# A two-layer diffusion backbone: the first projections by contraction tile, the second MLP half on normalised input, the output stores on two queues

## The chip, the cores and the metric

The kernel runs on 1 core of a Trainium2 chip. The metric is device time in microseconds (us) from the first to the last instruction of a launch, as a median of 3 runs: 902.71 us before (902.44 to 903.71). About 0.2% (1.8 us) is what a measurement of this kernel can tell from no change.

## The reference

384 tokens (128 context, 256 latent) of width 1024 pass two layers. In each layer, for both token groups with their own modulation vectors:

```
mod = silu(c) @ w_mod[d] + b_mod[d]          # six vectors of 1024: sa, ca, ga, sm, cm, gm
h   = rmsnorm(x, norm_mix) * (1 + ca) + sa
q, k, v, gb, gc, xin, u, vs = split(h @ w_in[d])
x  += ga * (concat(diff_attention, gated_conv, chunk_mlp) @ w_out[d])
h   = rmsnorm(x, norm_mlp) * (1 + cm) + sm
x  += gm * (relu(h @ w_up[d])**2 @ w_down[d])   # hidden width 4096
```

A last RMSNorm gives the outputs `y`; the context keys and values of both layers are outputs too. All weights are float32 in HBM.

## The kernel before

**Products.** Every weight tile (128 x 1024 float32, 512 KB) is loaded into a ring of six `raw` buffers, rounded by ScalarE to `whi` (L201), and VectorE puts the rest into `wlo` (L203). Activations lie transposed, as 8 tiles `kt` of 128 features by 384 tokens, in the same two pieces (`hh`, `hl`). One product is then three matmuls (`mm3`, L220 to L222). `whi` and `wlo` have four buffers each.

**Two kinds of `hh`, `hl`.** "Raw" input is `x` times its per-feature scale, without the norm's factor `rstd`, which is multiplied in after the product; the shift vector is carried as two more columns (TE = 386), so that its product comes with the others as a bias. "Normed" input has norm and shift in it (`normed`, L355). Both have a row pitch of 386 elements, whether 384 or 386 columns are read. The first projections of a layer and all up projections of the MLP read raw input; the other projections read normed input. In the MLP (two halves f of 16 hidden tiles: up `pup`, then down `pdn`), `hidden` takes the bias columns to `ub`, multiplies by `rstd` on VectorE, then has ReLU with bias, square and rounding on ScalarE.

**The modulation vectors.** The vectors of layer 0 but the last come from TensorE (`mod_products`: `pm` from `raw` and `sct`, L262), the rest from VectorE (`mod_sums`, `junk`, 112 products of 128 x 1024, L315). The first one (the scale of layer 0's norm) is needed before anything can be projected; it is made in 4 parts of two feature tiles.

**The start.** Key and query of heads 0 and 1 (four accumulators `pkq`) are built first: four whole weight tiles are loaded and split, then two feature tiles at a time are scaled as the parts of the vector come, and each accumulator takes its products for these two. Products of the next vectors stand between them.

**The order.** Engines run their own streams in the order in which the Python code records instructions. Side work is kept as generators: a heap releases a step when a counter of "ticks" (one for each product of three matmuls) has come far enough; the table `WAIT` holds the distances, a pair for the two layers. SyncE (SP) issues all loads and stores; its order is left to the scheduler.

**Softmax, layer by layer.** `attention(h, u)`: scores `sc` (three PSUM buffers `misc` shared with the transposes `pt`), negated maxima `nm` (VectorE), exponentials `e` (ScalarE), scaling and combining (`s`, `e`), transposes `pt`, copies `ats`, value products `po`. Beside it `keys` and `queries` rotate and split: `rt`, `kh`, `qs` and `kl`.

**The end.** The last down tile is done for latent tokens (256 columns) and then for context tokens (128): residual (L969), square, mean over features (`pstat`), ScalarE's logarithm and exponential, a refinement (L341 to L343), then four multiplies of two feature tiles each (three on VectorE, one on GpSimd, L988), each stored by SP (L989).

Of the kernel before, what the change touches and what calls it, by code (L numbers as in the profile page):

```python
# [9 lines left out]
F32 = mybir.dt.float32  # L10
# [5 lines left out]
P = 128  # L16
# [14 lines left out]
PARTS = 4  # L31
# [4 lines left out]
    "sums_down": (5, 0),  # L36
    "hid0": (1, 3),
    "hid1": (3, 4),
    "later": (4, 4),
    "later2": (4, 6),  # L40
    "spread": (1, 0),
    "final": (4, 3, 3, 3),
    "rstd": (3, 10),
# [4 lines left out]
    "at4": (5, 5),  # L48
    "at5": (1, 3),
    "at6": (2, 2),  # L50
    "at7": (3, 3),
    "at8": (2, 3),
    "at9": (2, 2),
    "at10": (3, 4),
    "at11": (2, 1),
    "at12": (2, 3),
    "k0": (1, 3),
    "k1": (9, 6),
    "k2": (1, 3),
    "q0": (1, 1),  # L60
    "q1": (5, 6),
    "q2": (2, 4),
    "fh0": (8, 14),
    "fh1": (2, 5),
    "fh2": (2, 2),
    "fh3": (5, 5),
    "cv0": (1, 5),
    "cv1": (2, 2),
    "cv2": (2, 3),
    "cm0": (1, 1),  # L70
    "sy": (4, 1),
    "normed": (3, 3),
    "wait_normed": (2, 12),
    "mix": (4, 4),
    "heads": (4, 1),
    "mods": (7, 0),
    "mods0": (2, 1),
    "sums": (7, 0),
    "sums0": (61, 1),
# [21 lines left out]
def dit_kernel(ctx, tc, xT, cT, wmod, wmodT, wall, ck, cv, ws, lam, bs_in, small, rope, ident_in, yT, kT_out, v_out):  # L101
# [10 lines left out]

    ahead = wpool.tile([P, 1024], F32, tag="raw", name="raw", bufs=6)
    nc.sync.dma_start(ahead, wmod[0, 0])
    c_sb = const.tile([P, KT, 2], F32, name="c_sb")
    nc.sync.dma_start(c_sb, cT)
# [130 lines left out]
    def mod_products():  # L247

        for i, (d, v) in enumerate(MOD_PE):
            pm = ps.tile([P, 256], F32, tag="mod", name="pm", bufs=1)  # L250
            tr = work.tile([P, KT, 32], F32, name="tr", tag="rtmp", bufs=1)

            n = per = PARTS if i == 0 else 1
            width = 256 // n
            for f in range(n):
                own = slice(f * width, f * width + width)
                for q in range(KT // per):
                    w = ahead if (i, f, q) == (0, 0, 0) else raw_chunk(wmod[i, f * KT // per + q])
# [10 lines left out]
                    if n > 1 or q % 2 == 1:  # L269
                        yield  # L270
                dts = slice(f * KT // n, (f + 1) * KT // n)
# [4 lines left out]
    hh = const.tile([P, KT, TE], F32R, name="hh")  # L276
    hl = const.tile([P, KT, TE], F32R, name="hl")
# [78 lines left out]
    def normed(scale, shift, every):  # L356
# [11 lines left out]
        for dt in range(KT):  # L368
            for g, a, b in GROUPS:
                nc.scalar.activation(hh[:, dt, a:b], t[:, a:b], AF.Identity, bias=shift[:, dt, g : g + 1])  # L370
            ahead = times(dt + 1) if dt + 1 < KT else None
            for g, a, b in GROUPS:
                nc.vector.scalar_tensor_tensor(
                    hl[:, dt, a:b], t[:, a:b], shift[:, dt, g : g + 1], hh[:, dt, a:b].bitcast(F32),
                    ALU.add, ALU.subtract,
                )
# [4 lines left out]
    def scaled_high(dt, scale):  # L381

        for g, a, b in GROUPS:
            nc.scalar.activation(hh[:, dt, a:b], x[:, dt, a:b], AF.Identity, scale=scale[:, dt, g : g + 1])

    def scaled_low(dt, scale):
        for g, a, b in GROUPS:
            nc.vector.scalar_tensor_tensor(  # L388
                hl[:, dt, a:b], x[:, dt, a:b], scale[:, dt, g : g + 1], hh[:, dt, a:b].bitcast(F32),
# [67 lines left out]
    def shift_products(raws, bias, t0, t1):  # L457
# [3 lines left out]
        for r in range(2):  # L461
            for j in range(4):
                kt = 4 * r + j
                mm(pb[32 * j : 32 * j + 32, 0 : n * P], sh[:, kt, :], raws[:, t0:t1, kt * P : kt * P + P],
# [44 lines left out]
    for d in range(DEPTH):  # L509
        lay = d * S_LAYER  # L510
        wt = {name: waits[d] for name, waits in WAIT.items() if len(waits) == DEPTH}
        a = (hh, hl)
# [26 lines left out]
        if d == 0:  # L539
            raws = wpool.tile([P, 2 * NPRE[d], 1024], F32, tag="hidH", name="raws")  # L540
            w2 = [refill(raws[:, i]) for i in range(2 * NPRE[d])]
            spread = spread_silu()

            def load_raw(i):
                nc.sync.dma_start(raws[:, i], wall[i])

            def split(i):
                next(w2[i])
                next(w2[i], None)

            def scaled(dt):
                scaled_high(dt, amix[d])
                scaled_low(dt, amix[d])
# [4 lines left out]
            next(products)  # L558
            nc.sync.dma_start(sm, small)
            next(products)  # L560
            load_raw(0)
            load_x(0)
# [549 lines left out]
```

## Time and profile before

| | |
|---|---|
| median of 3 runs | 902.71 us (902.44 to 903.71) |
| profiled execution, own time | 903.88 us |
| its span, first to last instruction | 902.1 us |
| TensorE busy | 876.5 us (97%) |
| VectorE, ScalarE, GpSimd busy | 653.7, 479.6, 83.5 us |
| mean granted clock of TensorE | 0.994 |

Rows of the windows view give, for a stretch in us from the span's start, its length and each engine's busy time with its instruction count, then the granted TensorE clock (1.00 is full), the DMA engines' busy share and GB/s. Timeline rows give start, duration, engine, line, operation and tiles, and in brackets the idle time of the engine before it and what ended it. Group rows end in busy time and mean duration in ns.

### The profile page before, as it was taken

The page shows a single profiled execution, that of the slowest core. Times are in us where ns is not written, and L with a number is a line of the kernel's source. Part 1 is how long each engine was busy: PE and PEld are TensorE (multiplying, and loading weights), DVE is VectorE, ACT ScalarE, POOL GpSimd, SP SyncE. Part 2 cuts the span into 40 slices and gives each one's busy share as a digit, 9 for nine tenths or more (in the row PEclk, how much of TensorE's full clock was granted, in tenths as well). Part 3 has the DMA queues.
Part 4 walks back from the last instruction along what each step waited for, and adds up shares of the span by engine and source line. Part 5 has one row for each costly group of instructions (what it writes and reads, how often), then busy time and mean ns, then how long its engine had stood idle before and what let it go on. Part 6 is the DMA issues. An engine that isn't in the chain of part 4 may idle for free.

```text
span 902.1 us, 14515 instructions
## 1 busy us (share of the span) xinstructions
PE 876.5 (97%) x5476; PEld 843.3 (93%) x5476; DVE 653.7 (72%) x1214; ACT 479.6 (53%) x949; POOL 83.5 (9%) x84
## 2 busy tenths in 40 slices
PE   5999999999999999999999989999999999999996
PEld 4877889999999999999997889999999999999995
DVE  4698888899888878889979877568886344554433
ACT  4568665547652236653446777545765223665331
POOL 1014210030000000000112430002000000000021
PEclk9999999999999999999999999999999999999998
DMA  9887784455656665566763323233555433333302
GB/s 342 318 310 261 250 277 169 137 165 189 208 191 231 211 211 183 187 204 216 230 199 123 111 81 110 95 109 127 192 201 166 134 123 120 137 118 121 113 1 70
DMA packets 48470, 156.55 MB, mean 174 GB/s; under 512 B 5392, under 2 KB 11024, under 8 KB 48400
## 3 DMA queue, kind: packets, MB, share of 16 engines
q1 hardware_dynamic: 48400, 155.63, 51.4%
q8 instruction: 43, 0.70, 0.3%
q14 instruction: 27, 0.22, 0.1%
HBM read 152.98 MB, written 2.62 MB: 172 GB/s over the span
## 4 chain that ended last, share of the span: by engine, by line
PE 86%; DVE 6%; ACT 3%; issue 2%; DMA 1%; POOL 1%; SPq 0%; DVEq 0%; ACTq 0%; POOLq 0%
PE pdn L221 10%; PE pdn L222 10%; PE pdn L220 10%; PE pup L221 10%; PE pup L220 10%; PE pup L222 9%; PE po L222 2%; PE po L221 2%; PE po L220 2%; PE pm L262 2%; PE pkq L220 2%; PE pkq L221 2%; DVE wlo L203 2%; PE pkq L222 1%; PE po L786 1%
## 5 line engine op out<-in xcount | busy, mean ns | idle before, releaser
L201 ACT CAST whi<-raw 128x1024 fp32r<-128x1024 f32 x182 | 190.1, 1051 | 302.9 <-PE pdn L221 154.0
L203 DVE TENSOR_TENSOR wlo<-raw,whi 128x1024 fp32r<-128x1024 f32 x182 | 223.6, 1234 | 63.6 <-ACT whi L201 63.5
L220 PE MATMUL pdn<-ah,whi 128*128 128x384 f32 (+2 forms) x528 | 174.7, 331 | 0.0
L221 PE MATMUL pdn<-al,whi 128*128 128x384 f32 (+2 forms) x528 | 174.6, 331 | 0.0
L222 PE MATMUL pdn<-ah,wlo 128*128 128x384 f32 (+2 forms) x528 | 174.6, 331 | 0.0
L220 PE MATMUL pup<-hh,whi 128*128 128x386 f32 x512 | 174.2, 340 | 0.0
L221 PE MATMUL pup<-hl,whi 128*128 128x386 f32 x512 | 173.7, 339 | 0.3
L222 PE MATMUL pup<-hh,wlo 128*128 128x386 f32 x512 | 172.8, 338 | 0.0
L315 DVE SCALAR_TENSOR_TENSOR junk<-raw,cb 128x1024 bf16<-128x1024 f32 x112 | 137.4, 1227 | 0.4
L221 PEld LDWEIGHTS pdn<-al,whi 128*128 128x128 f32 x528 | 99.2, 188 | 0.0
L220 PEld LDWEIGHTS pdn<-ah,whi 128*128 128x128 f32 x528 | 99.2, 188 | 0.0
L222 PEld LDWEIGHTS pdn<-ah,wlo 128*128 128x128 f32 x528 | 99.2, 188 | 0.0
L221 PEld LDWEIGHTS pup<-hl,whi 128*128 128x128 f32 x512 | 96.9, 189 | 1.1 <-DVE hl L388 0.9
L220 PEld LDWEIGHTS pup<-hh,whi 128*128 128x128 f32 x512 | 96.4, 188 | 0.3
L222 PEld LDWEIGHTS pup<-hh,wlo 128*128 128x128 f32 x512 | 96.5, 188 | 0.0
L337 POOL TENSOR_TENSOR sacc<-sacc,sq 128x384 f32<-128x384 f32 x23 | 29.4, 1279 | 667.9 <-ACT sq L330 595.4
L927 ACT ACTIVATE relu<-relu,ub 128x128 f32<-128x128 f32 (+1 forms) x128 | 51.0, 445 | 8.7 <-DVE relu L924 8.7
L399 DVE SCALAR_TENSOR_TENSOR x<-pdn,modv,x 128x128 f32<-128x128 f32 (+1 forms) x62 | 23.0, 413 | 43.9 <-PE pdn L222 43.9
L931 DVE TENSOR_TENSOR al<-relu,ah 128x384 fp32r<-128x384 f32 x64 | 35.4, 554 | 11.8 <-ACT ah L929 11.6
L220 PE MATMUL po<-y,whi 128*128 128x384 f32 x128 | 43.0, 336 | 0.0
L923 DVE COPY ub<-pup 128x2 f32<-128x2 f32 x64 | 10.2, 159 | 45.0 <-PE pup L222 44.4
L222 PE MATMUL po<-y,wlo 128*128 128x384 f32 x128 | 42.8, 334 | 0.0
(202 smaller groups left out, 1448.5 us busy)
## 6 DMA issues: line engine op xcount, KB each, us to landing
raw<-in_wall_dram SPq DMA_DIRECT2D x182, 512.0 KB, 3.6
raw<-in_wmodT_dram SPq DMA_DIRECT2D x56, 512.0 KB, 4.2
raw<-in_wmod_dram SPq DMA_DIRECT2D x40, 512.0 KB, 5.9
raws<-in_wall_dram SPq DMA_DIRECT2D x6, 512.0 KB, 7.8
x<-in_xT_dram SPq DMA_DIRECT2D x8, 192.0 KB, 7.6
out_dram<-x SPq DMA_DIRECT2D x4, 256.0 KB, 2.6
mix<-in_cv_dram SPq DMA_DIRECT2D x2, 256.0 KB, 4.5
mix<-in_ws_dram SPq DMA_DIRECT2D x2, 256.0 KB, 5.1
```

Source lines behind the costliest of these rows:

```text
L201: nc.scalar.copy(hi, r)
L203: nc.vector.tensor_sub(lo, r, hi.bitcast(F32))
L220: mm(out, wh[wsl], ah[asl], start=first, stop=False)
L221: mm(out, wh[wsl], al[asl], start=False, stop=False)
L222: mm(out, wl[wsl], ah[asl], start=False, stop=last)
L262: mm(pm[32 * j : 32 * j + 32, own], sct[:, kt, :], w[:, (4 * k + j) * width : (4 * k + j + 1) * width], start=(kt == 0), stop=(kt == KT - 1),)
L315: nc.vector.scalar_tensor_tensor(junk, w, 1.0, cb[:, g], ALU.mult, ALU.mult, accum_out=mr[:, dt, g : g + 1])
L337: eng.tensor_add(stat["acc"], stat["acc"], sq)
L399: nc.vector.scalar_tensor_tensor(x[:, dt, a:b], pacc[:, a:b], gate[:, dt, g : g + 1], x[:, dt, a:b], ALU.mult, ALU.add)
L923: nc.vector.tensor_copy(ub, pt[:, T:TE])
L927: nc.scalar.activation(r[:, s0:s1], r[:, s0:s1], AF.Relu, bias=ub[:, g : g + 1])
L931: nc.vector.tensor_sub(al[:, i], r, ah[:, i].bitcast(F32))
```

## The change

- **Pitch.** `hh` and `hl` get two views: raw with 386 columns a tile, as before, and normed (`nh`, `nl`) with 384, packed at 384 in the same memory. The first projections of layer 0, which need no bias columns, read and write the packed view too.
- **Second MLP half.** While the down projection of the first half runs, the MLP input is made once more, normalised and shifted (`normed_again`: for each of 8 tiles two scale, two shift and two rest instructions on VectorE and ScalarE, on 128 and 256 columns). The second half's up projection then reads 384 columns instead of 386, and its `hidden` is ReLU from PSUM, square and rounding on ScalarE and the rest on VectorE: no `ub`, no multiply by `rstd`, no bias.
- **Start.** The four first weight tiles are stored by feature tile of the contraction (`wfirst`: 8 transfers of 256 KB in place of 4 of 512 KB). The loop goes over `kt`: split a 128 x 512 piece, scale one tile of `x`, and give all four accumulators their product. The first vector comes in parts of 1, 1, 2 and 4 feature tiles. The shift vector's products stand inside this loop after `kt` 5. Before it, TensorE runs 8 and 5 matmuls on a constant whose result nobody reads. `c` is loaded ahead of the first modulation tile.
- **VectorE's modulation products.** Of layer 0's 80 in the MLP, 16 and 24 in the first half become 16 and 12; 16 and 24 in the second become 28 (every 4 ticks) and 24.
- **Table.** Some 30 entries of `WAIT` change.
- **End.** The order of the latent group's multiplies is 0, 4, 6, 2 (two on GpSimd), that of the context group 0, 4, 2, 6; two of the context group's stores are issued by ScalarE.

```diff
-PARTS = 4
+PARTS = (1, 1, 2, 4)
 WAIT = {
-    "later": (4, 4),
+    "later": (2, 3),
-    "k0": (1, 3),
+    "k0": (1, 5),
-    "q0": (1, 1),
-    "q1": (5, 6),
+    "q0": (2, 2),
+    "q1": (5, 7),
-    "wait_normed": (2, 12),
+    "wait_normed": (13, 13),
...
-    hh = const.tile([P, KT, TE], F32R, name="hh")
-    hl = const.tile([P, KT, TE], F32R, name="hl")
+    parts_of_x = [const.tile([P, KT * TE], F32R, name=n) for n in ("hh", "hl")]
+    hh, hl = raw_x = [t.rearrange("p (k t) -> p k t", k=KT) for t in parts_of_x]
+    nh, nl = normed_x = [t[:, 0 : KT * T].rearrange("p (k t) -> p k t", k=KT) for t in parts_of_x]
...
+    def normed_again(scale, shift, every):
+        for dt in range(KT):
+            t = temp("t")
+            for g, a, b in GROUPS:
+                nc.vector.scalar_tensor_tensor(
+                    t[:, a:b], x[:, dt, a:b], scale[:, dt, g : g + 1], stat["rstd"][:, a:b], ALU.mult, ALU.mult
+                )
+            yield every[0]
+            for g, a, b in GROUPS:
+                nc.scalar.activation(nh[:, dt, a:b], t[:, a:b], AF.Identity, bias=shift[:, dt, g : g + 1])
+            yield every[1]
+            for g, a, b in GROUPS:
+                nc.vector.scalar_tensor_tensor(
+                    nl[:, dt, a:b], t[:, a:b], shift[:, dt, g : g + 1], nh[:, dt, a:b].bitcast(F32),
+                    ALU.add, ALU.subtract,
+                )
+            yield every[2]
...
+            warm(8)
             next(products)
             nc.sync.dma_start(sm, small)
+            load_x(0)
+            warm(5)
             next(products)
+            scaled_high(0, amix[d], normed_x)
+            scaled_low(0, amix[d], normed_x)
+            w = split(0)
+            for kt in range(KT):
+                ahead_w = None
+                for i in range(n):
+                    pre_step(i, kt, w)
+                    if (kt, i) in ((5, 3), (6, 1), (6, 3), (7, 1), (7, 3)):
                         next(products)
+                    if kt == KT - 1:
+                        continue
+                    if i == 0:
+                        if kt in (0, 1, 3):
+                            next(products)
+                        ahead_w = split(kt + 1)
+                    elif i == 1:
+                        if kt in (0, 1, 3):
+                            next(products)
+                        scaled_high(kt + 1, amix[d], normed_x)
+                        scaled_low(kt + 1, amix[d], normed_x)
...
+                if f == 1:
+                    nc.scalar.activation(r, pt[:, 0:T], AF.Relu)
+                    nc.scalar.activation(r, r, AF.Square)
+                    nc.scalar.copy(ah[:, i], r)
+                    yield wt["hid1"]
+                    nc.vector.tensor_sub(al[:, i], r, ah[:, i].bitcast(F32))
+                    return
...
-                go(hidden(i, proj_tiles(a, 1, TE, "pup")))
+                go(hidden(i, proj_tiles(a, 1, T, "pup") if f else proj_tiles(raw_x, 1, TE, "pup")))
...
-        for k in range(0, KT, 2):
-            eng = nc.gpsimd if k == 4 else nc.vector
+        for k, eng, queue_of, wait in (
+            ((0, nc.vector, nc.sync, 1), (4, nc.gpsimd, nc.sync, 1), (6, nc.gpsimd, nc.sync, 5), (2, nc.vector, nc.sync, 1))
+            if g == 1
+            else ((0, nc.vector, nc.sync, 1), (4, nc.gpsimd, nc.scalar, 1), (2, nc.vector, nc.scalar, 1), (6, nc.vector, nc.sync, 1))
+        ):
```

**Where instructions move, first place: TensorE at the start.** Before (`pm` are products of the first vector, `pkq` those of keys and queries):

```order
L262 MATMUL pm<-raw,sct 32x64 x32
L220 MATMUL pkq<-hh,whi 128x384
L221 MATMUL pkq<-hl,whi 128x384
L222 MATMUL pkq<-hh,wlo 128x384
L220 MATMUL pkq<-hh,whi 128x384
```

and with the change:

```order
L599 MATMUL pkq<-ones_d 128x128 x8
L264 MATMUL pm<-raw,sct 32x32 x32
L599 MATMUL pkq<-ones_d 128x128 x5
L220 MATMUL pkq<-hh,whi 128x384
L221 MATMUL pkq<-hl,whi 128x384
L222 MATMUL pkq<-hh,wlo 128x384
L264 MATMUL pm<-raw,sct 32x32 x32
L220 MATMUL pkq<-hh,whi 128x384
```

The first part of the vector needs one 512 KB tile instead of two, the second part stands behind only three `pkq` matmuls, and 13 unread products stand ahead.

**Second place: ScalarE in layer 1,** where the last block of head 0's softmax meets the first of head 1's, after the query projection of head 2 (`kh`, `qs` are splits of that head's key and query, `e` the exponentials and their scaling, `ats` the transposed weights that head 0's `po` waits for). Before:

```order
L726 ACTIVATE mix<-pq 128x256
L674 CAST kh<-mix 64x384 x2
L751 ACTIVATE e,s<-sc,nm 128x128 x2
L677 CAST kh<-mix 64x384 x2
L757 ACTIVATE e<-e,s 128x128
L690 CAST qs<-mix 64x256 x2
L774 COPY ats<-pt 128x3x128
```

and with the change:

```order
L763 ACTIVATE mix<-pq 128x256
L788 ACTIVATE e,s<-sc,nm 128x128 x2
L711 CAST kh<-mix 64x384 x2
L794 ACTIVATE e<-e,s 128x128
L714 CAST kh<-mix 64x384 x2
L811 COPY ats<-pt 128x3x128
```

The exponentials pass the key's splits, and `ats` passes the query's splits. VectorE's stream has the same move: `nm` and `s` pass the pair `kl`.

**Third place: VectorE at the end** (L969 and L1015 are the residual, L988 and L1038 the multiplies by `rstd`). Before:

```order
L343 SCALAR_TENSOR_TENSOR rstd<-rtmp,rstd 128x256
L988 TENSOR_TENSOR x<-x,rstd 128x2x256 x2
L969 SCALAR_TENSOR_TENSOR x<-pdn,modv_92,x 128x128
L988 TENSOR_TENSOR x<-x,rstd 128x2x256
L341 TENSOR_TENSOR rtmp<-rstd 128x128
```

and with the change:

```order
L350 SCALAR_TENSOR_TENSOR rstd<-rtmp,rstd 128x256
L1038 TENSOR_TENSOR x<-x,rstd 128x2x256
L1015 SCALAR_TENSOR_TENSOR x<-pdn,modv_92,x 128x128
L1038 TENSOR_TENSOR x<-x,rstd 128x2x256
L348 TENSOR_TENSOR rtmp<-rstd 128x128
```

One multiply of the latent group stands ahead of the context group's residual instead of two; the other has gone to GpSimd.

More of the change, by code (lines that the diff above doesn't have):

```diff
@@ L251, in mod_products @@
             tr = work.tile([P, KT, 32], F32, name="tr", tag="rtmp", bufs=1)
[L253 to L258, printed above, removed]
+            pieces = tuple((sum(PARTS[:f]), m) for f, m in enumerate(PARTS)) if i == 0 else ((0, KT),)
+            for t0, m in pieces:
+                own = slice(32 * t0, 32 * (t0 + m))
+                width = 32 * m
+                per = KT // m
+                for q in range(m):
+                    w = ahead if (i, t0, q) == (0, 0, 0) else raw_chunk(wmod[i, t0 + q])
                     for k in range(per):
@@ L539, in dit_kernel @@
         if d == 0:
-            raws = wpool.tile([P, 2 * NPRE[d], 1024], F32, tag="hidH", name="raws")
-            w2 = [refill(raws[:, i]) for i in range(2 * NPRE[d])]
-            spread = spread_silu()
[L544 to L553, printed above, removed]
+            n = 4
@@ L556, in load_x, with split @@
                 nc.sync.dma_start(x[:, dt], xT[:, dt])
+            def split(kt):
+                nc.sync.dma_start(raw4[:, kt], wfirst[kt])
+                hi = wpool.tile([P, 1024], F32R, tag="whi", name="whi", bufs=4)
+                lo = wpool.tile([P, 1024], F32R, tag="wlo", name="wlo", bufs=4)
+                pieces = (0, 2, 4) if kt == 0 else (0, 4)
+                for p0, p1 in zip(pieces, pieces[1:]):
+                    cols = slice(p0 * P, p1 * P)
+                    nc.scalar.copy(hi[:, cols], raw4[:, kt, cols])
+                    nc.vector.tensor_sub(lo[:, cols], raw4[:, kt, cols], hi[:, cols].bitcast(F32))
+                return hi, lo
@@ L602, in shifted @@
             def shifted():
-                yield from steps(products, KT // 2 + 1, 4)
                 nc.vector.tensor_copy(sh[:, :, 0:2], modv[0][:, 0])
@@ L943, in dit_kernel @@
             if d == 0:
-                start(steps(sums, 24, wt["sums_down"]), 2)
+                start(steps(sums, (12, 24)[f], (9, 5)[f]), 2)
+            if f == 0:
+                start(normed_again(amlp[d], modv[d][:, 3], (2, 2, 12)), 3)
             def down(pt, w, c, cols):
@@ L1027, in _pack @@
     d, v = MOD_PE[0]
[L1028 to L1029 removed]
+    first = []
+    for f, m in enumerate(PARTS):
+        t0 = sum(PARTS[:f])
+        part = wm[d, :, :, v, t0 : t0 + m].reshape(m, KT // m, P, m, 4, 32).transpose(0, 2, 1, 4, 3, 5)
+        first.append(part.reshape(m, P, 1024))
+    mods[0] = np.concatenate(first)
     out["wmod"] = np.stack(mods)
```

169 lines of the change are left out of this document (80 added, 89 removed).

## The prediction

> **What bounds the kernel now.** I read the page first, then the windows, then what TensorE waited for, then the timelines where it waited. The page's span and TensorE's busy time:
>
> ```profile
> span 902.1 us, 14515 instructions
> PE 876.5 (97%) x5476; PEld 843.3 (93%) x5476; DVE 653.7 (72%) x1214; ACT 479.6 (53%) x949; POOL 83.5 (9%) x84
> ```
>
> TensorE is idle for 902.1 - 876.5 = 25.6 us, so a gain has two sources only: those 25.6 us, and matmuls that take less time each. The windows show where the idle time lies (the columns behind the length are PE, PEld, DVE, ACT, POOL):
>
> ```profile
> 0.00:25.00 25.00, 14.80 (x228) 11.98 (x229) 11.68 (x32) 9.79 (x18) 2.97 (x11) 1.00 0.93 348
> 25.00:50.00 25.00, 25.00 (x237) 20.71 (x236) 17.43 (x40) 12.81 (x25) 0.00 (x0) 1.00 0.87 316
> 50.00:100.00 50.00, 49.51 (x351) 37.42 (x350) 44.76 (x109) 39.65 (x91) 16.38 (x18) 1.00 0.78 284
> ...
> 335.00:395.00 60.00, 60.00 (x343) 60.00 (x342) 48.09 (x86) 39.79 (x72) 0.00 (x0) 1.00 0.56 184
> 265.00:325.00 60.00, 60.00 (x348) 60.00 (x347) 49.72 (x78) 15.19 (x15) 0.00 (x0) 1.00 0.68 224
> 490.00:500.00 10.00, 8.08 (x31) 6.30 (x30) 9.87 (x18) 7.12 (x16) 6.08 (x6) 0.83 0.34 113
> 500.00:520.00 20.00, 18.31 (x105) 17.14 (x104) 16.68 (x35) 15.96 (x41) 8.51 (x9) 1.00 0.41 129
> 520.00:540.00 20.00, 17.73 (x112) 17.11 (x110) 15.52 (x33) 15.04 (x41) 6.04 (x6) 1.00 0.22 76
> 890.00:902.10 12.10, 3.55 (x27) 3.06 (x25) 6.75 (x13) 1.30 (x5) 2.74 (x2) 0.67 0.42 130
> ```
>
> 10.2 us are lost in the first 25, 8.6 in the last 12, and 1.9 + 1.7 + 2.3 = 5.9 in layer 1's attention from 490 to 540. The MLP (335 to 395 is an up, 265 to 325 a down projection) has no idle time at all. TensorE's waits, in total us, times and longest:
>
> ```profile
> PE pkq L220 <- ACT hh L384: 2.8, 2, 1.9
> PE nat L451 <- DVE hl L373: 1.9, 1, 1.9
> PE sc L741 <- ACT e L751: 1.7, 1, 1.7
> PE po L786 <- ACT ats L774: 1.4, 2, 1.2
> PE pt L763 <- DVE e L759: 1.1, 1, 1.1
> ```
>
> **The second MLP half: 2.1 us.** TensorE is full there, so only the time of a matmul counts. The last instruction of a window runs some 0.34 us over its end: an up matmul comes every 60.34 / 343 = 175.9 ns, a down matmul every 60.34 / 348 = 173.4 ns. Both windows have one kind alone, 386 columns at a pitch of 386 in the first, 384 at 384 in the second. The new second half is 384 at 384, like the down projection. It has 2 layers x 16 tiles x 24 = 768 matmuls: 768 x 2.5 = 1.9 us; the count is good to one instruction in 343, which is 0.5 ns, so 1.5 to 2.4. I take 2.1 for what goes with the first tiles' waits.
>
> What hides the new normalisation: TensorE's 66 us of down projection, in which VectorE has 60 - 49.7 = 10.3 us free in 60, and 12 products of 1227 ns leave the stage in layer 0:
>
> ```profile
> L315 DVE SCALAR_TENSOR_TENSOR junk<-raw,cb 128x1024 bf16<-128x1024 f32 x112 | 137.4, 1227 | 0.4
> L924 DVE TENSOR_TENSOR relu<-pup,rstd 128x384 f32<-128x384 f32 x64 | 35.0, 548 | 0.1
> L923 DVE COPY ub<-pup 128x2 f32<-128x2 f32 x64 | 10.2, 159 | 45.0 <-PE pup L222 44.4
> ```
>
> and in VectorE's timeline, the same steps (scale, rest) where layer 1's mixer makes its normed input:
>
> ```profile
> 477.13 1.40 DVE L362 SCALAR_TENSOR_TENSOR t<-x,amix,rstd 128x128 f32<-128x128 f32 x4
> 478.44 0.74 DVE L373 SCALAR_TENSOR_TENSOR hl<-t,modv,hh 128x128 fp32r<-128x128 f32 x2
> ```
>
> By these two rows a tile costs 0.70 + 0.74 (four and two instructions under one row, so 0.35 and 0.37 each), eight of them 11.5 us, against 14.7 that leave. In layer 0's second up projection 12 products come (14.7 us), and 16 times the copy and the multiply go (0.159 + 0.548, 11.3 us): VectorE goes from 48.1 to about 51 in 60. Cover gone would cost the excess over 60, and there is none by 9 us. ScalarE does one ReLU for two.
>
> **The packed view elsewhere: 1.0 us.** The normed projections of the mixer stand between other work, so no window has them alone; the groups by form do (last figure: mean ns of one):
>
> ```profile
> L221 PE MATMUL pup<-hl,whi 128*128 128x386 f32 x512 | 173.7, 339 | 0.3
> L221 PE MATMUL pu<-hl,whi 128*128 128x384 f32 x32 | 10.8, 338 | 0.0
> L221 PE MATMUL po<-y,whi 128*128 128x384 f32 x128 | 42.8, 334 | 0.0
> ```
>
> `pu` has 384 columns like `po`, but reads at pitch 386, and takes 4 ns longer; `pup`, two columns wider, only 1 ns more than that. So most of the 2.5 ns is the pitch, and about 2 ns of it comes back in each of 12 tiles x 24 = 288 matmuls a layer: 0.6 us in layer 0, where TensorE is the bound, and 0.4 of 0.6 in layer 1, where it partly waits.
>
> The Trainium skill (TensorE: Matmul & The Clock Gate, Back-to-back issue gap) has the time go with the columns alone, plus a fixed 2.5 ns, at 2.4 GHz; by it two columns are 0.8 ns of a matmul, and this term would be nothing. By that rule `pu` and `po` would be alike; the rows disagree, and the sum keeps the rows.
>
> **The start: 1.6 us.** The marker in TensorE's timeline is the first value projection `nat`; all 144 `pkq` matmuls, the shift vector's products and `pb` stand before it, then as now.
>
> ```profile
> 5.47 1.08 PE L262 MATMUL pm<-raw,sct 128*32 128x64 f32 x32 [5.47 <-DVE sct L136]
> 10.88 0.69 PE L220 MATMUL pkq<-hh,whi 128*128 128x384 f32 x1 [1.95 <-ACT hh L384]
> 12.58 0.52 PE L222 MATMUL pkq<-hh,wlo 128*128 128x384 f32 x1
> 17.16 0.33 PE L222 MATMUL pkq<-hh,wlo 128*128 128x384 f32 x1
> 51.98 0.39 PE L449 MATMUL nat<-whi,hh 128*128 128x512 f32 x1
> ```
>
> and two rows of the DMA issues:
>
> ```profile
> raw<-in_wmod_dram SPq DMA_DIRECT2D x40, 512.0 KB, 5.9
> x<-in_xT_dram SPq DMA_DIRECT2D x8, 192.0 KB, 7.6
> ```
>
> With half the data for the first part, `pkq` starts near 8 us instead of 10.88 (512 KB less is 1.5 us at the window's 348 GB/s, half the `pm` 0.5, half the pieces to scale and split an estimated 0.8), and at the full rate (0.52 us falls to 0.33 only by 17 us now; the unread products take that phase). But the work then catches up with the transfers. Up to the shift vector's last tile the queue moves 16 x 512 KB of vectors, 8 x 192 of `x`, 2048 of first weights, 1024 of two more and 149 small: 12,949 KB = 13.26 MB. 348 GB/s give 8.70 MB by 25 us; the other 4.56 MB take 13.1 us at 348, 14.4 at 316, 16.1 at 284: the last tile lands at 38.1, 39.4 or 41.1. In TensorE's new stream half a pair of products (0.5), 54 `pkq` (9.4) and up to 1.7 us of `pb` and statistics remain behind it. With 38.7 us, between the two measured rates, `nat` starts at 50.4: a gain of 1.6. The bounds: 284 GB/s gives 52.7, a loss of 0.7; transfers that never bind give (51.98 - 12.58) - 1.9 (a wait for `hh`) - 1.8 (slow phase) = 35.7 us of work from 8.1 on, `nat` at 43.8, a gain of 8.2.
>
> **Layer 1's softmax: 2.5 us.** VectorE's and ScalarE's timelines at the first two waits:
>
> ```profile
> 501.35 1.54 DVE L678 TENSOR_TENSOR kl<-mix,kh 64x384 fp32r<-64x384 f32 x2
> 521.25 0.80 ACT L690 CAST qs<-mix 64x256 fp32r<-64x256 f32 x2
> ```
>
> At each place the instruction ahead now stands behind: `kl` before `nm` (1.5 of the 1.7 us), `qs` before `ats` and `kh` before `e` (all 1.4), `kl` before `s` (some 0.7 of 1.1, since the next `e` stays behind `kl`). At most 3.6. What moved back is late next: `kl` and `qs` are wanted by the scores of the next block, one tile of 4.2 us later. I take 2.5, and zero as the other end. The wait of `nat` (1.9) stays: as many splits and normalising steps stand before that `hl` as did.
>
> It costs more than itself. The clock is 0.83 in 490 to 500, which is 10 x 0.17 x 2 = 3.4 us at half speed, 1.7 us lost. The Trainium skill (TensorE: Matmul & The Clock Gate, Part 1) has the clock fall after an idle window of about 3.4 us; by that a wait of 1.9 would cost no clock. The row says it did, and the loss stays in the sum.
>
> **The end: 1.5 us.**
>
> ```profile
> 892.21 0.27 PE L222 MATMUL pdn<-ah,wlo 128*128 128x128 f32 x1
> 891.12 2.38 DVE L988 TENSOR_TENSOR x<-x,rstd 128x512 f32<-128x512 f32 x2
> 893.41 0.34 DVE L969 SCALAR_TENSOR_TENSOR x<-pdn,modv,x 128x128 f32<-128x128 f32 x1
> 896.67 1.62 DVE L988 TENSOR_TENSOR x<-x,rstd 128x256 f32<-128x256 f32 x3
> 896.71 0.96 POOL L988 TENSOR_TENSOR x<-x,rstd 128x256 f32<-128x256 f32 x1 [3.77 <-DVE rstd L343]
> 897.70 1.96 SPq L989 DMA_DIRECT2D out_dram<-x  x4
> ```
>
> The context residual could start at 892.5 and waits for two multiplies until 893.4; with one (892.3) it gains 0.85. The stores are issued 0.49 apart, the first only behind GpSimd's multiply (897.67), the last at 899.2; on two queues the last waits for the last multiply alone, 898.3 - 0.85 = 897.4: 1.75 in all, if nothing else slows. GpSimd's second multiply may: the two VectorE multiplies beside it took 1.19 each. I take 1.5, from 0.7 to 2.2.
>
> **Sum.** 1.6 + 2.1 + 1.0 + 2.5 + 1.5 = 8.7 us, so a span of 893.4. The profiled execution's own time is 1.8 over its span, the median 0.6: **894.0 us**.
>
> **Rivals.**
> - *Only the columns count:* a matmul's time falls by 2 of 386 columns, 175.9 x 2 / 386 = 0.9 ns, so 0.9 x 768 = 0.7 in place of 2.1 + 1.0: 896.4. Against it stand `pu` and `po`; for it, that they are means of durations. 12%. The rule that the Trainium skill has for the gap (named above) is this rival.
> - *The softmax waits come back a block later*: 0 in place of 2.5: 896.5. VectorE's 16.7 and ScalarE's 16.0 of 20 us speak for it. 17%.
> - *The transfers never bind at the start*: 8.2 in place of 1.6: 887.4. Against: they are busy 0.93 already. 10%.
> - *Slower: the clock falls at the start.* TensorE now waits for raw tiles between short runs of matmuls, some ten times from 9 to 39 us. If each drops the clock as in 490 to 500 (1.7 us), six drops (10.2) outweigh the 8.7, and eight give 902.7 - 8.7 + 13.6 = 907.6. Against: the waits are 0.3 to 1.5 us by the rate above, and waiting for data the clock costs nothing. 5%.
> - *No change in sum* (several terms at their low ends, the start at a loss): about 902. 5%.
>
> My forecast has 51%. **Range 889.5 to 898.5**, which holds both 896s and half of the fast start. Faster by over 0.2% (1.8 us, what this kernel's measurement can tell) 0.89, within it 0.06, slower 0.05.
>
> **What would show it.** Windows of the second up projection at 346 to 348 matmuls in 60 us, `pu` at 334 ns; `nat` first at 50.4 and TensorE waiting for `raw` before it; the waits of `sc`, `po` and `pt` gone from the list, that of `nat` still there; the last store issued 1.5 us nearer to the last `pdn`. Wrong it would be by VectorE rows `hl` or `wlo` in TensorE's list for the MLP, or by a granted clock under 0.9 between 10 and 40 us.

## The result, and the profile after

| | before | changed |
|---|---|---|
| median | 903.21 us (902.44 to 904.42, 4 runs) | 897.25 us (896.73 to 897.44, 4 runs) |
| ratio | | 0.9933, 95% interval 0.9920 to 0.9947 |
| profiled execution, own time | 903.88 us | 896.73 us |
| its span | 902.1 us | 894.9 us |

The change is faster, by 0.67% (6.0 us by the medians, 7.15 us by the two profiled executions). Forecast were 894.0 us and a range of 889.5 to 898.5. The page's first rows of the changed kernel, and its windows (length; PE, PEld, DVE, ACT, POOL; clock, DMA share, GB/s):

```profile
span 894.9 us, 14560 instructions
PE 875.6 (98%) x5502; PEld 840.4 (94%) x5502; DVE 657.3 (73%) x1218; ACT 485.7 (54%) x954; POOL 82.8 (9%) x85
```

```profile
0.00:25.00 25.00, 20.46 (x331) 16.85 (x331) 12.17 (x37) 10.43 (x24) 3.00 (x11) 1.00 0.94 347
25.00:50.00 25.00, 23.97 (x170) 18.97 (x169) 18.05 (x40) 13.78 (x27) 0.00 (x0) 1.00 1.01 384
...
330.00:390.00 60.00, 60.00 (x347) 60.00 (x346) 56.35 (x86) 35.09 (x57) 0.00 (x0) 1.00 0.80 249
490.00:500.00 10.00, 7.51 (x32) 5.26 (x31) 9.86 (x21) 6.96 (x16) 5.00 (x6) 1.00 0.34 112
500.00:520.00 20.00, 18.35 (x110) 17.37 (x111) 17.52 (x35) 17.36 (x45) 7.60 (x9) 1.00 0.38 122
520.00:540.00 20.00, 20.00 (x128) 19.87 (x127) 16.24 (x37) 15.97 (x48) 5.21 (x6) 1.00 0.35 102
```

TensorE's idle time falls from 25.6 to 19.3 us, although 13 of its matmuls are new and unread. The second up projection (330 to 390) has no idle time and 347 matmuls in 60 us, against 342 or 343 before; VectorE there is at 56 of 60, so the cover for the new work holds, but thinner than forecast (51). What TensorE waits for now:

```profile
PE pkq L220 <- ACT hh L410: 2.3, 3, 1.0
PE nat L477 <- DVE hl L380: 2.3, 3, 1.5
PE pt L800 <- DVE e L796: 1.4, 1, 1.4
PE sc L778 <- ACT e L788: 1.1, 2, 0.9
PE pkq L599 <- DVE ones_d L123: 1.1, 1, 1.1
PE pm L264 <- DMA raw<-in_wmod_dram: 0.9, 2, 0.6
PE psb L498 <- ACT shb L494: 0.9, 1, 0.9
```

The starts of TensorE's first and last instruction of each stage, taken from the two traces, split the 7.13 us of span (902.07 and 894.94 to the hundredth):

| stretch on TensorE, us | before | changed | difference |
|---|---|---|---|
| span's start to the first value projection of layer 0 | 51.98 | 50.29 | -1.69 |
| to layer 0's first up projection (mixer) | 141.40 | 141.44 | +0.04 |
| first MLP half, layer 0 | 135.31 | 135.29 | -0.02 |
| second up projection, layer 0 | 67.72 | 66.77 | -0.95 |
| down projection, layer 1's first products | 84.15 | 84.14 | -0.01 |
| layer 1, first value projection to first output projection | 104.94 | 102.82 | -2.12 |
| to the second up projection of layer 1 | 168.93 | 168.94 | +0.01 |
| second up projection, layer 1 | 67.72 | 66.77 | -0.95 |
| down projection to its last matmul | 70.06 | 70.05 | -0.01 |
| last matmul to the span's end | 9.86 | 8.43 | -1.43 |

From the first value projection to the last matmul these distances repeat far better than whole runs do: in the runs below that leave a stretch alone, it comes out within some 0.05 us. They are the measure used here. The two ends repeat less well, and each figure for them is one execution's: with the start's instructions and addresses untouched, the first value projection starts at 50.25 to 50.83 us (50.5 to 51.6 where only buffers moved), and the last stretch takes 8.16 to 8.45 us with the same instructions in it.

### The profile page after: what moved, and what is told of

It is laid out like the page before. It is cut to its first block, busy times and chain, and to the rows that moved or that the text cites. A ratio compares the mean times of both kernels' runs of the same rounds, so it can differ in the third digit from the quotient of the medians.

```text
span 894.9 us, 14560 instructions
## 1 busy us (share of the span) xinstructions
PE 875.6 (98%) x5502; PEld 840.4 (94%) x5502; DVE 657.3 (73%) x1218; ACT 485.7 (54%) x954; POOL 82.8 (9%) x85
## 4 chain that ended last, share of the span: by engine, by line
PE 85%; DVE 6%; DMA 5%; issue 2%; ACT 1%; SPq 0%; POOL 0%; DVEq 0%; POOLq 0%; ACTq 0%
PE pdn L221 10%; PE pdn L220 10%; PE pdn L222 10%; PE pup L221 10%; PE pup L220 10%; PE pup L222 10%; PE po L221 2%; PE po L222 2%; PE po L220 2%; DMA raw<-in_wmod_dram 2%; PE po L823 1%; DVE wlo L203 1%; PE pm L264 1%; DVE hl L380 1%; DMA raw<-in_wall_dram 1%
## 5 line engine op out<-in xcount | busy, mean ns | idle before, releaser
L220 PE MATMUL pup<-hh,whi 128*128 128x386 f32 (+1 forms) x512 | 173.7, 339 | 0.0
L221 PE MATMUL pup<-hl,whi 128*128 128x386 f32 (+1 forms) x512 | 172.8, 337 | 0.3
L222 PE MATMUL pup<-hh,wlo 128*128 128x386 f32 (+1 forms) x512 | 172.5, 337 | 0.0
L220 PE MATMUL po<-y,whi 128*128 128x384 f32 x128 | 43.1, 337 | 0.0
L221 PE MATMUL po<-y,whi 128*128 128x384 f32 x128 | 42.8, 334 | 0.0
L477 PE MATMUL nat<-whi,hl 128*128 128x512 f32 (+1 forms) x96 | 33.1, 345 | 2.4 <-DVE hl L380 2.3
L475 PE MATMUL nat<-whi,hh 128*128 128x512 f32 (+1 forms) x96 | 33.9, 354 | 0.5 <-ACT hh L377 0.5
```

What stands on the lines that cost most here:

```text
L220: mm(out, wh[wsl], ah[asl], start=first, stop=False)
L221: mm(out, wh[wsl], al[asl], start=False, stop=False)
L222: mm(out, wl[wsl], ah[asl], start=False, stop=last)
L475: mm(o, ah, wh[:, cols], start=(kt == 0 and tt % n == 0), stop=False)
L477: mm(o, al, wh[:, cols], start=False, stop=(kt == KT - 1 and (tt % n == n - 1 or tt == 2)))
```

## The experiments

Each is the changed kernel with one edit, its distances set beside the changed kernel's (its median 897.25 us). The kernel before had medians of 903.2 to 903.7 us beside them.

### 1. The second half on raw input again

```
-  start(steps(sums, (16, 28)[f], (8, 4)[f]), 2)
+  start(steps(sums, 16, 8), 2)
...
-  start(normed_again(amlp[d], modv[d][:, 3], (2, 2, 12)), 3)
...
-  go(hidden(i, proj_tiles(a, 1, T, "pup") if f else proj_tiles(raw_x, 1, TE, "pup")))
+  go(hidden(i, proj_tiles(raw_x, 1, TE, "pup")))
```

> The changed kernel with its second MLP half as before: raw input of 386 columns, no second normalisation, VectorE's 80 products again as 16, 24, 16, 24. By the stage marks of the changed kernel each second up projection became 0.95 us shorter (67.72 to 66.77 us in layer 0). Theory (matmul spacing alone): both come back, the matmul spacing there is 176.3 ns in place of 173.9, the span grows by 1.9 us over 894.9, and nothing else moves by more than 0.2. Rival (only the two columns count): 0.7 us. Rival (the new normalisation delays something in the down projection or the table's other places): less than 1.9 or a gain.

Measured: 899.10 us (898.97 to 899.64), ratio to before 0.9954 (0.9942 to 0.9967). (`hidden` of the second half has the bias and the multiply by `rstd` again, and VectorE's products are divided as before.) Both second up projections are 0.95 us longer; every other distance from the first value projection to the last matmul is within 0.05 us. The edit's worth is 1.9 us, all of it in how often a matmul starts; the down projection that now carries the normalisation pays nothing.

### 2. The normed view at pitch 386

```
-  nh, nl = normed_x = [t[:, 0 : KT * T].rearrange("p (k t) -> p k t", k=KT) for t in parts_of_x]
+  nh, nl = normed_x = [t[:, :, 0:T] for t in raw_x]
```

> The changed kernel with the normed view at a row pitch of 386 again, 384 columns read: the pitch alone is undone, the columns stay. Theory (pitch and columns both count): the second half's spacing goes from 173.9 to about 175.5 ns, as the mixer's 384 columns at pitch 386 had before, 768 x 1.6 = 1.2 us, and the normed projections of the mixer (576 matmuls) give back 1.2 ns each, 0.7 us: 1.9 us in all. Rival (only columns count, as the Trainium skill has it): spacing 173.9 and no change of the time. Rival (only the pitch counts): 176.3 and 3.3 us.

Measured: 899.24 us (899.01 to 899.37), ratio 0.9954 (0.9941 to 0.9966). The windows of the second up projection (PE alone) with 386 columns at 386 (run 1), 384 at 386 (this run) and 384 at 384 (the changed kernel's row above, x347):

```profile
330.00:390.00 60.00, 60.00 (x342) 1.00 0.58 184
```

```profile
330.00:390.00 60.00, 60.00 (x344) 1.00 0.78 241
```

The mean distance between starts is 176.4, 175.3 and 173.9 ns: of the 2.5 ns, 1.1 go with the two columns and 1.4 with the pitch (runs 9 to 12 have as much and more at a pitch of 384, by the addresses alone). Each second up projection is 0.54 us longer than at 384, the two mixers 0.24 and 0.29. "Only the columns count" falls: by it nothing would have changed.

### 3. Without the unread products

```
-  warm(8)
-  warm(5)
```

> The changed kernel without the 13 products that nobody reads. Theory (the transfers set the start): TensorE is at half speed until some 11 to 17 us, but it waits for the first vector's tiles anyway; the shift vector's last tile still lands near 38.3 us, and the first value projection starts at 50.3 to 50.8 us in place of 50.29: at most 0.5 us. Rival (TensorE's work sets it): the slow phase costs 0.15 to 0.2 us for each matmul in it, 1.5 to 3 us, and the value projection starts at 52 to 53 us.

Measured: 897.47 us (896.54 to 897.87); the first value projection starts at 50.35 us, and no later distance up to the last matmul differs by more than 0.05. TensorE's key and query matmuls ran slow until 14 us, as the durations in this run's timeline show:

```profile
13.87 0.52 PE L222 MATMUL pkq<-hh,wlo 128*128 128x384 f32 x1
...
16.68 0.34 PE L221 MATMUL pkq<-hl,whi 128*128 128x384 f32 x1
16.86 0.34 PE L222 MATMUL pkq<-hh,wlo 128*128 128x384 f32 x1
17.03 0.44 PE L220 MATMUL pkq<-hh,whi 128*128 128x384 f32 x1
```

In the changed kernel they take 0.34 from 9.6 us on, and it gains nothing: TensorE waits until 17.00 us there for the same matmul that starts at 17.03 here. The 13 products are worth nothing.

### 4. Layer 1's table entries as before

```
...
-  "later": (2, 3), "at9": (2, 3), "k0": (1, 5), "q0": (2, 2), "q1": (5, 7), "wait_normed": (13, 13),
+  "later": (2, 4), "at9": (2, 2), "k0": (1, 3), "q0": (2, 1), "q1": (5, 6), "wait_normed": (13, 12),
```

> The changed kernel with layer 1's table entries as before (later 4, at9 2, k0 3, q0 1, q1 6, wait_normed 12). Layer 1 from its first value projection to the first output projection took 104.9 us before and 102.8 with the change. Theory (the moved softmax steps): the waits of scores, value products and transposes come back as before (1.7, 1.2, 1.1 us against 1.1 and 1.4 in the changed kernel), 104.4 us, a loss of some 1.6 us whether or not the clock falls near 494 us. Rival (the change had a clock that did not fall there, by luck): without a fall of the clock no more than 0.5 us is lost, and with one 1.2 to 1.7 us.

Measured: 899.11 us (898.58 to 900.59), ratio 0.9954 (0.9942 to 0.9967); layer 1's stretch 104.80 us, 1.98 more than in the changed kernel, with a clock that is full throughout. The waits of this run:

```profile
PE sc L778 <- ACT e L788: 2.6, 1, 2.6
PE nat L477 <- DVE hl L380: 2.1, 2, 1.9
...
PE po L823 <- ACT ats L811: 1.3, 1, 1.3
PE pt L800 <- DVE e L796: 1.1, 1, 1.1
```

So these six entries, which move the softmax steps, are worth 2.0 us, and it was not luck with the clock. The rows show one thing more. Before, the clock was at half for 3.4 us here (494.74 to 498.16 in the trace) and the wait for scores was 1.7 us; at full clock the same order waits 2.6. The stretch took 104.94 us with the half clock and 104.80 without it, although the packed view alone is worth 0.29 there (run 2). So the time lost to the clock had been hidden: TensorE only came later to a wait that VectorE and ScalarE end.

### 5. One queue for the last stores

```
-  (4, nc.gpsimd, nc.scalar, 1), (2, nc.vector, nc.scalar, 1)
+  (4, nc.gpsimd, nc.sync, 1), (2, nc.vector, nc.sync, 1)
```

> The changed kernel with all four context stores on one queue again. From the last down matmul's start to the span's end it takes 8.39 us in the changed kernel and took 9.89 before; the last store is issued 4.92 us after that matmul, 7.01 before. Prediction's step (the issues 0.49 apart set the end): one queue issues at 0, 0.49, 0.98 and 1.47 us from the first, the last at 5.2 us behind the matmul, and 0.3 to 0.9 us of the 1.5 goes. Rival (the landings, some 0.5 us apart whatever the queue, set the end): 0 to 0.2 us.

Measured: 897.67 us (897.21 to 898.09), 8.76 us from the last matmul to the end in place of 8.43. The traces have the last store landing 7.72 us behind the last matmul, 7.23 in the changed kernel and 8.92 before; from that landing to the span's end it takes 0.94 to 1.21 us more, differently from one execution of the same instructions to the next. By the landing the second queue is worth 0.5 us and the whole change 1.7. In the changed kernel the last store is issued 2.09 us sooner behind the last matmul than before (4.92 against 7.01), but it lands 2.3 us after that in place of 1.9: with one queue (before and in this run) the four context stores landed 0.50 to 0.55 us apart, with two 0.32 to 0.56.

### 6. The latent group's multiplies in the old order

```
-  ((0, nc.vector, nc.sync, 1), (4, nc.gpsimd, nc.sync, 1), (6, nc.gpsimd, nc.sync, 5), (2, nc.vector, nc.sync, 1))
+  ((0, nc.vector, nc.sync, 1), (2, nc.vector, nc.sync, 1), (4, nc.gpsimd, nc.sync, 1), (6, nc.vector, nc.sync, 1))
```

> The changed kernel with the latent group's multiplies in the old order, two of VectorE's ahead of the context residual and one on GpSimd; the context group as changed. Prediction's step: the residual starts 0.85 us later and the end with it, 9.2 us from the last down matmul's start to the end in place of 8.39. Rival (the four context multiplies and stores set the end anyway): no more than 0.3.

Measured: 898.93 us (898.33 to 899.05); 9.87 us from the last matmul to the end, and the last landing at 8.67. The timelines of VectorE (and GpSimd), this run first, the changed kernel second:

```profile
885.61 2.97 DVE L1038 TENSOR_TENSOR x<-x,rstd 128x512 f32<-128x512 f32 x3
888.50 0.34 DVE L1015 SCALAR_TENSOR_TENSOR x<-pdn,modv,x 128x128 f32<-128x128 f32 x1
```

```profile
885.42 0.69 DVE L1038 TENSOR_TENSOR x<-x,rstd 128x512 f32<-128x512 f32 x1
885.47 3.45 POOL L1038 TENSOR_TENSOR x<-x,rstd 128x512 f32<-128x512 f32 x2 [8.05 <-DVE rstd L350]
886.82 0.35 DVE L1015 SCALAR_TENSOR_TENSOR x<-pdn,modv,x 128x128 f32<-128x128 f32 x1 [0.70 <-PE pdn L222]
```

The expectation spoke of two multiplies ahead of the residual; the shorter distances of this table put all three there. The residual then starts 1.80 us behind the last matmul instead of 0.31, and the last landing, like the end, moves by 1.44: about 0.7 us for each multiply in the residual's way, and the queues give almost nothing of it back.

### 7. Half of the shift vector's loads

```
+  if i != 1 or q % 2 == 0:
       w = ahead if (i, t0, q) == (0, 0, 0) else raw_chunk(wmod[i, t0 + q])
```

Four tiles are left out and the others used twice, so the shift vector and the output are others.

> The changed kernel, but four of the eight 512 KB tiles of the shift vector are not loaded: each of the others is used twice, so this vector is not the reference's and the output neither. Every product stays. Theory (the transfers set the start up to the shift vector's last tile, TensorE's work from there): 2.1 MB less at some 385 GB/s lets that tile land 5.4 us sooner, near 33 us, and the first value projection starts at 45 to 46.5 us in place of 50.29. Rival (TensorE's or the splits' work sets it): 49.8 or later. After that the distance to the later stages stays as it was.

Measured: 895.60 us (2 runs); the shift vector's last tile lands at 33.9 us in place of 38.3, but the first value projection starts at 49.55, only 0.74 us sooner than in the changed kernel's trace, and 0.7 to 1.3 sooner than in those with the start untouched. As the only bound, the transfers up to that tile fall. They are the first one, though: in the traces of the changed kernel and of the ten runs that keep the loads and products of the shift vector whole, that tile lands at 38.25 to 39.49 us, and `nat` starts 12.00 to 12.09 us behind it in every one. Here it starts 15.65 behind: once the tile lands some 0.7 us sooner, something else sets the start.

### 8. The same vector without those products too

```
-  for q in range(m):
+  for q in (0, 2, 4, 7) if i == 1 else range(m):
...
-  if i > 0 and q % 2 == 1:
+  if i > 1 and q % 2 == 1 or i == 1:
```

Loads and products of four of the eight tiles are left out.

> The changed kernel without four of the eight 512 KB tiles of the shift vector and without their products, so that this vector and the output are not the reference's. Without the loads alone the first value projection came at 49.55 us in place of 50.29. Theory (TensorE's own work sets it from some 25 us on): the four products of some 0.65 us each go as well, 2.6 us, and the value projection starts near 47.0. Rival (statistics, normalisation and splits on VectorE and ScalarE set it): 49.0 to 49.6, with TensorE waiting for the missing time.

Measured: 894.51 us (one run); the value projection starts at 48.37 us, 1.92 sooner. Its waits ahead of that:

```profile
PE pkq L220 <- ACT hh L410: 2.3, 3, 1.0
PE pm L264 <- DMA raw<-in_wmod_dram: 1.6, 3, 0.7
```

Of the 2.6 us of products that went, 1.2 came through; the waits for tiles grew from 0.3 (run 7) to 1.6. Neither side alone sets this stretch. In the changed kernel TensorE is busy 23.97 of 25 us from 25 to 50, and the share of the DMA engines is 1.01; take much from one, and the other holds.

### 9 and 10. Where the two pieces of x lie in memory

Run 9 puts unused columns ahead of both pieces, so that they begin where the weights begin, modulo 2048 bytes:

```
-  parts_of_x = [const.tile([P, KT * TE], F32R, name=n) for n in ("hh", "hl")]
+  parts_of_x = []
+  for n, lead, tail in (("hh", 448, 0), ("hl", 496, 80)):
+      whole = const.tile([P, lead + KT * TE + tail], F32R, name=n)
+      parts_of_x.append(whole[:, lead : lead + KT * TE])
```

> The changed kernel with unused columns ahead of the two pieces of x, so that both begin at the same address modulo 2048 bytes (672) at which the weight pieces, the hidden activations of the down projection and the mixer's output begin; before they begin at 928 and 992. Pitch, columns and work stay. Theory A (the time of a matmul goes with where its moving rows lie against the weights that are loaded beside it): the second half's up matmuls go from 173.89 to 173.34 ns as the down matmuls have, the mixer's from about 174.7 to 173.4, the first half's (pitch 386, off by 8 bytes more for each feature tile) from 176.35 to 174.2 to 176.3: faster by 0.4 + 0.7 us at least, by 2.8 at most. Theory B (pitch and columns alone): no change.

Run 10 has `("hh", 0, 0), ("hl", 1008, 16)` instead.

> The changed kernel with the second piece of x 16,384 bytes behind the first, in place of 12,352, so that both begin at 928 modulo 2048, and the weights at 672 as before. Theory A (position against the weights): the second half stays between 173.9 and 176 ns, no gain. Theory A2 (position of the two pieces against each other, as the down projection's two pieces lie a multiple of 4096 apart): 173.34 there, and a gain as in the run before. Theory B (pitch and columns alone): no change.

Measured: 896.54 us (896.07 to 897.21) and 896.48 us (896.25 to 896.53), ratios 0.9925 (0.9912 to 0.9939) and 0.9925 (0.9911 to 0.9938). In both the second up projection has 348 matmuls in 60 us, 173.34 ns each, exactly the down projection's; from the first value projection to the last matmul both take 0.70 us less than the changed kernel. The first half (386 columns at pitch 386) stays at 176.35. That addresses count is shown: nothing else was changed. (The 0.7 us are read from the distances; the medians differ by as much, but that is less than a measurement of whole runs can tell.) Run 10 speaks for the position of the two pieces against each other, since both lie 256 bytes off the weights modulo 2048.

### 11 and 12. The raw view at pitches of 400 and 512

```
+PITCH = 400
...
-  parts_of_x = [const.tile([P, KT * TE], F32R, name=n) for n in ("hh", "hl")]
-  hh, hl = raw_x = [t.rearrange("p (k t) -> p k t", k=KT) for t in parts_of_x]
+  parts_of_x = [const.tile([P, KT * PITCH], F32R, name=n) for n in ("hh", "hl")]
+  hh, hl = raw_x = [t.rearrange("p (k t) -> p k t", k=KT)[:, :, 0:TE] for t in parts_of_x]
```

Run 11 has 400, run 12 has 512.

> The changed kernel with the raw view (386 columns) at a row pitch of 400 elements in place of 386; the normed view stays at 384. Changes the address of each feature tile and nothing of the work. Theory (what the pitch of 386 costs is its alignment: 400 x 4 bytes is a multiple of 64 as 384 x 4 is): the first half's up matmuls go from 176.35 to about 175.0 ns, 768 x 1.35 = 1.0 us, and layer 1's 96 raw key and query matmuls 0.1 us more: 1.1 us faster, a version better than the change. Rival (only a packed view is fast, or the time goes with the columns): no change.

> The changed kernel with each raw piece of x at a row pitch of 512 elements: the second piece then begins 16,384 bytes behind the first and every feature tile of the raw view a multiple of 2048 bytes from every other; the normed view stays packed at 384. Theory (where consecutive moving tiles begin against each other, modulo 2048 bytes, adds up to 3 ns to a matmul): the second half stays at 173.34 ns as in the run before, and the first half's matmuls of 386 columns go from 176.35 to 173.34 + 2 / 2.2 = 174.2 ns; 768 + 96 of them save 1.8 us, the time falls to some 894.7 us, better than both kernels. Rival (a row of 386 columns is slow wherever it lies): the first half stays at 176.3 or above and the time at the 896.5 us of the run before.

Measured: 900.12 us (899.53 to 901.34) with 400, 899.87 us (899.37 to 900.87) with 512: 2.9 and 2.6 us slower than the changed kernel. The raw half goes to 177.1 and 176.7 ns, and the normed half, whose code and pitch nobody touched, to 176.0. The second up projection of run 10 and of the run with 512:

```profile
330.00:390.00 60.00, 60.00 (x348) 60.00 (x348) 56.33 (x86) 35.26 (x57) 0.00 (x0) 1.00 0.81 250
```

```profile
330.00:390.00 60.00, 60.00 (x343) 60.00 (x342) 57.42 (x86) 34.43 (x56) 0.00 (x0) 1.00 0.77 239
```

Two of the groups by form (last figure: mean ns) of the changed kernel, of run 10 and of the run with 512, where all lines stand one lower:

```profile
L220 PE MATMUL pup<-hh,whi 128*128 128x384 f32 x256 | 86.2, 337 | 0.0
L222 PE MATMUL pup<-hh,wlo 128*128 128x384 f32 x256 | 86.0, 336 | 0.0
```

```profile
L220 PE MATMUL pup<-hh,whi 128*128 128x384 f32 x256 | 85.6, 334 | 0.0
L222 PE MATMUL pup<-hh,wlo 128*128 128x384 f32 x256 | 85.6, 334 | 0.0
```

```profile
L221 PE MATMUL pup<-hh,whi 128*128 128x384 f32 x256 | 86.5, 338 | 0.0
L223 PE MATMUL pup<-hh,wlo 128*128 128x384 f32 x256 | 86.5, 338 | 0.0
```

With 512 the first piece begins at the same address as in run 10, the second 16,384 bytes behind it as there, and the normed view has the same pitch; and yet the matmuls are 2.7 ns slower. So neither the place of the pieces nor their position against each other sets this alone. What differs is the place of the buffers behind them, the weights' among them, which the larger tiles push back by 3,968 bytes. Those of the down projection move along with the weights, and its matmuls stay at 173.4 ns. Of what these runs change, that leaves where x lies against the weights. The kernels' memory maps give the distance of each piece from the weight pieces, modulo 256 bytes:

| normed half, 384 columns | hh | hl | ns a matmul |
|---|---|---|---|
| down projection, every run (`ah`, `al`) | 0 | 0 | 173.34 |
| run 9; run 10 | 0 | 0 | 173.34 |
| changed kernel | 0 | 64 | 173.89 |
| run 2 (8 bytes more each feature tile) | 0 to 56 | 64 to 120 | 175.28 |
| pitch 400; pitch 512 | 128 | 128 | 176.0 |

That the mean time goes with this distance fits all five rows, those of run 10 included, where 256 bytes modulo 2048 are 0 modulo 256. It was read from these runs after they were made, and no run was made to test it: a raw view of pitch 512 with 128 bytes more ahead of the weights would have been that test. Two things in the traces speak against the distance as a rule for a single matmul. Within run 2 the step from one start to the next, as a mean for each feature tile and piece, goes from 169 to 184 ns in no order of the distance. And in run 11 the raw feature tiles of 386 columns lie 128, 192, 0 and 64 bytes off in turn; the mean steps behind matmuls at 0, 64, 128 and 192 are 177.4, 177.3, 176.2 and 177.3 ns, so a distance of 0 gains nothing there. So these runs leave the place against the weights, and which property of it counts stays open. The fastest kernel with the reference's output is run 10, 0.8 us under the changed kernel by the medians.

## Why the prediction was right, and where not

The sign and the range held. The sum was 8.7 us, the two profiled spans differ by 7.13; term by term:

- **The start, 1.6: measured 1.69, from one execution of each kernel.** The forecast start of `nat` was 50.4, the measured 50.29. The mechanism held: the step "the last tile lands at 38.7, and 11.7 us of work remain" describes what eleven traces show (landing at 38.25 to 39.49, 12.0 us behind it in each). That the size came out so close is luck, twice over. The landing was worked out with 4.56 MB behind 25 us at a rate between 316 and 348 GB/s; the windows view of the changed kernel has 405 GB/s there, and so some 5.4 MB, and the two errors cancel (the same columns as in the windows above):

```profile
25.00:38.26 13.26, 12.39 (x96) 8.29 (x97) 7.98 (x20) 7.52 (x17) 0.00 (x0) 1.00 1.03 405
```

  And the profiled execution of the changed kernel is the fastest of its four, while that of before lies 0.7 us above its median. By the medians (6.0 us, of which 5.4 lie behind the start in the table above) some 0.5 us are left for the start, and up to 1.0 by the medians of before that stand beside the experiments; this is an estimate.

  The other bound, "transfers that never bind", was set too low, at 43.8. It took 35.7 us of work from the first key and query matmuls on, counted from 12.58 us, where the third of them starts, and took every later matmul at full rate, while the timeline has the first matmuls behind each product of a vector slower:

```profile
13.07 1.13 PE L264 MATMUL pm<-raw,sct 128*32 128x64 f32 x64
14.13 0.44 PE L220 MATMUL pkq<-hh,whi 128*128 128x384 f32 x1
17.00 0.45 PE L220 MATMUL pkq<-hh,whi 128*128 128x384 f32 x1 [1.03 <-ACT hh L410]
...
50.29 0.50 PE L475 MATMUL nat<-whi,hh 128*128 128x512 f32 x1 [0.45 <-ACT hh L377]
```

  Run 7 still waits 2.4 us for `hh` and 0.3 for raw tiles; without these waits `nat` would start near 46.9 there, an estimate, so the rival "the transfers never bind" (887.4) was 3 us too fast even with the transfers away. The forecast sign "TensorE waiting for `raw`" came in part: 0.9 us for raw tiles and 2.3 for `hh` in the changed kernel's trace, 2.6 and 1.4 in run 5's, whose start is the same.
- **The second MLP half, 2.1: measured 1.9.** The step's own arithmetic, 768 x 2.5 ns, was exact; the 0.2 added for the first tiles' waits did not exist. VectorE's cover held, though at 56 of 60 where 51 were forecast.
- **The packed view elsewhere, 1.0: measured at most 0.5.** The packed view is worth 0.24 and 0.29 us in the two mixers (run 2). The step that failed is "about 2 ns of it comes back": `pu` went from 338 to 336 or 337 ns, not to the 334 of `po`. Pitch was not all that `pu` and `po` differ in: `po` reads operands that lie alike with the weights, and `hl` begins 64 bytes off them in both kernels. Nor is that the whole of it: with both pieces alike (runs 9 and 10) `pu` still takes 335 or 336 ns, and what keeps it there is not shown. In layer 0 even this gain does not show (+0.04). Two delays that the prediction left out lie in that stretch: `nat`'s first three matmuls take 0.42 us longer (51.17 - 50.29 against 52.44 - 51.98), and `psb` waits 0.9 in place of 0.5. Together they are more than the packed view gives there, so something else gave time back; what it was, no run shows.
- **Layer 1's softmax, 2.5: measured 2.0** (run 4). The forecast that the waits of `sc`, `po` and `pt` go was half right: `po` is gone from the list, `sc` is at 1.1 (1.7 before) and `pt` at 1.4 (1.1 before). That is the rival "the waits come back a block later" for two of the three, in part. That `nat`'s wait stays was right (1.9 then, 2.3 now). The clock's loss that "stays in the sum" was neither there in the changed kernel's trace nor worth its 1.7 us before: run 4 has it swallowed by the next wait.
- **The end, 1.5: measured 1.43,** from the steps: the residual 0.89 us nearer to the last matmul (0.85 forecast), the last store issued 2.09 nearer where 1.75 was forecast, and landing 1.7 nearer. Of that, 0.27 went again behind the last landing, where executions of the same instructions differ by as much. The step "on two queues the last waits for the last multiply alone" was right for the issue and missed the landing. Alone, the queues are worth 0.5 by the landing (run 5).

So the span came out 1.5 us longer than forecast, and the median 3.25 us. By stretches, layer 0's mixer gave nothing where 0.6 stood in the sum, layer 1's attention 2.1 where 2.9 stood (softmax and packed view), the second half 1.9 where 2.1 stood. The other 1.7 lie in the step from span to median: 0.6 us over the span was taken from three runs of before, all of them faster than its profiled execution. The changed kernel's profiled execution was the fastest of its four, its median 2.3 over that span. A sum against one profiled execution carries that scatter, here as large as a whole term; the eleven starts above say that it lies mainly in when the shift vector's last tile lands.

Two rivals lie nearer to the measured median than the forecast does. Run 2 refutes the mechanism of "only the columns count" (896.4): 1.6 us of the gain come without a column less. Run 4 refutes the size of "the softmax waits come back" (896.5): 2.0 of the 2.5 us came. The Trainium skill (TensorE: Matmul & The Clock Gate, Back-to-back issue gap) gives the gap of an isolated matmul by its number of columns alone, and says that in a stream of weight loads and matmuls both set the spacing. These runs show 173.34, 173.89, 175.28 and 176.0 ns for the same 384 columns, each with a load of 128 columns of weights, at full clock. The rival of a clock that falls at the start did not come: in the changed kernel's timeline the key and query matmuls take 0.33 to 0.45 us each from 9.3 us to the first value projection. (The clock column cannot show it: it reads 1.00 for the first 25 us of before and of run 3 too, where they took 0.52 us until 16.4 and 13.9 us.)

## What to carry to other kernels

Where an engine is full, count its starts in windows of one kind of instruction: 342, 344 and 347 matmuls in 60 us told effects apart that durations blur. The count moves by one with where the window falls (346 and 347 in two windows of the changed kernel), so a finer difference needs the distance from a stage's first start to its last. Before pricing a transfer, ask what the engine would do without it: from 25 us on work and transfers were nearly level here, so that 4.4 us off the one gave 0.7. And compare an end that scatters over several executions before calling a forecast of it right. Compare stretch by stretch rather than whole runs, and treat a new tile size as an edit to every operand whose address moves with it.

## What the runs showed that was not expected

The time of a matmul depends on where its operands lie. The same 384 columns took from 173.34 to 176.0 ns, and enlarging one tile (pitch 400 or 512) made 768 matmuls slower whose own instructions and pitch did not change, 1.6 us of the 2.6 to 2.9 us that these kernels lost. Aligning both pieces gave 0.70 us on top of the change. The 386 columns of the first half, at 176.35 ns in every run with a pitch of 386, came down in none: they took 177.1 at 400, with every fourth tile at distance 0, and 176.7 at 512, with all tiles at 128. A run with all of them at 0 was not made.

A half clock of 3.4 us next to a wait cost almost nothing, and some 5 us more of slow matmuls at the start cost nothing that these runs can tell (50.35 us against 50.25 to 50.83): an engine that would have waited anyway lost no time by being slow.
